# Attention in a streaming-encoder layer: reciprocals of row sums made for two score tiles at once, and their probabilities halved behind the second's exponentials

## The chip, the cores and the metric

The kernel runs on one NeuronCore of a Trainium2 chip. A core has five instruction queues that run beside each other: PE (TensorE, matrix products; PEld are its weight loads), DVE (VectorE), ACT (ScalarE), POOL (GpSimd) and SP (SyncE, which here issues all transfers). Each queue is worked off in order, and an instruction that waits holds up what stands behind it on its queue. The metric is the device time of one execution in microseconds, the lower the better.

## The reference

One encoder layer with a sequence of 1024, a width of 1024 and one batch: a conditioning vector gives shift, scale and gate; two groups of eight heads attend side by side; a gated channel part with a causal convolution of width 3 follows. Cut to what the change is about:

```python
def mla_attention(q, k, v):                # latent attention: 8 heads, 96 wide
    # query blocks of 128; a key is seen if its chunk of 64 is not later than the query's
    s = einsum(q_block, k) * scale;  s = where(mask, s, -1e30)
    p = softmax(s);  return einsum(p, v)

def chunk_attention(q, k, v, rel_bias):    # chunk attention: 8 heads, 64 wide
    # chunks of 64 queries; each sees a band of its own chunk and the 8 before it
    s = einsum(q_chunk, k_band) * scale + bias(rel_bias)
    p = softmax(s);  return einsum(p, v_band)

mixed = concat([o_mla, o_ca]) @ w_out;  x = x + g_a * mixed
```

A softmax row is exp(s - max) divided by its sum. Everything is float32.

## The kernel before

**Number format.** Products are made in three passes: each operand is split into a high and a low half, and high x high, high x low and low x high are added. For the probabilities both halves are float16.

**Stages.** (1) The conditioning and the first projection (to about 85 us). (2) Chunk attention: 8 heads x 8 score tiles = 64 tiles, about 85 to 374 us. (3) Latent attention: 8 heads x 8 tiles = 64 tiles, about 401 to 624 us. (4) The output product and the channel part, from about 630 us to the end. A score tile is 128 queries of one head against all the keys that they may see. Tile i of a head is 128 x (i+1) wide in latent attention, up to 1024; in chunk attention it is 128, 256, 384, 512 and then 640 wide. Each head is worked in two units of four tiles.

**One score tile** (`Unit.scores`): PE makes the scores in PSUM (tag S, two buffers; L765 and L771). DVE masks and takes the row minimum of the negated scores (L778 to L786 in chunk attention; L789 and L790 in latent attention). ACT writes the exponentials to a tile P and their row sums to `rsum` (L797). P has three buffers for tiles up to 640 wide; wider ones use a pool of six pages. DVE makes the reciprocal of the row sum (L799) and multiplies it by a power of two, PSCALE (L800). For each piece of the tile (one piece, or two of at most 512 for latent tiles wider than 512) POOL writes the high half, P times the reciprocal, in float16 (L73, the helper `scale_pool`), DVE the low half, P times the reciprocal minus the high half (L819), both to a tile hl (four buffers, one latent piece in four elsewhere). Then SP issues one transposing transfer of both halves into a tile PT (L831).

**Value product** (`Unit.values`): for a pair of neighbouring tiles, an even one and the odd one behind it, PE multiplies the transposed halves with the values (L859). PT holds both tiles of the pair. After two pairs DVE and ACT combine the result (L868, L869) and SP stores it (L873).

**Order of the work.** The main loop goes over the 128 tiles. Step n makes the scores of tile n, and the value product of tile n-3 if that is the odd one of its pair. After each of the two, `pace` puts in work from a list of fillers in proportion to the PE time of the tile: projections during chunk attention, then the latent projection, the up-projections and the part of the output product that belongs to chunk attention. The instructions of each engine are then ordered by a planner with an estimated timeline: what is ready goes in the order of the program, but the blocks under `high_priority` count as further ahead by an offset, 400 places for scores and exponentials, 200 for the reciprocals, halves and transposes, 200 for the value products. That order is fixed when the program is built; at run time each queue only waits for what it needs.

The steps that the change touches are in these functions:

Of the kernel before, what the change touches and what calls it, by code (L numbers as in the profile page):

```python
# [13 lines left out]
F32 = mybir.dt.float32  # L14
# [4 lines left out]
AF = mybir.ActivationFunctionType  # L19
# [3 lines left out]
MUL, ADD, SUB, MIN, MAX = ALU.mult, ALU.add, ALU.subtract, ALU.min, ALU.max  # L23

P = 128
# [16 lines left out]
OFF_S, OFF_P, OFF_V = 400, 200, 200  # L42
# [3 lines left out]
PSCALE, VSCALE = 2.0 ** 15, 2.0 ** 14  # L46
# [18 lines left out]
def layer_kernel(ctx, tc, I, out):  # L65
    nc = tc.nc
    pe, act, dve, pool, sp = nc.tensor, nc.scalar, nc.vector, nc.gpsimd, nc.sync
# [4 lines left out]
    def scale_pool(o, i, s):  # L72
        pool.tensor_scalar(o, i, s, 1.0, op0=MUL, op1=MUL)  # L73
# [12 lines left out]
    cst = ctx.enter_context(tc.tile_pool(name="cst", bufs=1))  # L86
# [60 lines left out]
    def pgtile(shape, dt, name):  # L147
        return apg.tile(shape, dt, name=name, tag="pg", bufs=6)
# [585 lines left out]
    class Unit:  # L734
# [7 lines left out]
        def scores(u, i):  # L742

            qpg, kpgs = u.pages()
            bias = u.bias() if u.band else None
            lo = max(0, i - 4) if u.band else 0
            n = (i - lo + 1) * P
            nm = f"{u.nm}_{i}"
            rsum = cst.tile([P, 1], F32, name=f"rs{nm}", tag="rsum", bufs=4)
            ri = cst.tile([P, 1], F32, name=f"ri{nm}", tag="ri", bufs=4)  # L750
            with tc.high_priority(offset=OFF_S):
                s = ps.tile([P, 1024], F32, name=f"s{nm}", tag="S", bufs=2)
                n0 = max(0, min(4, i + 1) - lo) * P
                n1 = n - n0
                c0 = 512 - n0 if n1 else 0
                segs = [(c0, lo * P, n0, 0)] if n0 else []
                if n1:
                    segs.append((512, max(lo, 4) * P - 512, n1, 1))
                q = slice((i % 4) * P, (i % 4 + 1) * P)
                rs_ = slice(u.base, u.base + u.rows)  # L760
                if u.band:
                    qh, ql = qpg
                    for a, rr in ((qh[u.odd], slice(0, P)), (ql, rs_)):
                        for c, ko, w, kh in segs:
                            last = pe.matmul(s[:, c:c + w], a[rr, q], kpgs[kh][rr, u.odd, ko:ko + w],  # L765
                                             start=(a is not ql), stop=(a is ql))
                else:
                    for a in range(2):
                        for c, ko, w, kh in segs:
                            for b in range(2 - a):  # L770
                                last = pe.matmul(s[:, c:c + w], qpg[a][rs_, q], kpgs[kh][rs_, b, ko:ko + w],  # L771
                                                 start=(a == 0 and b == 0), stop=(a == 1))
                trail.append(last.ins)
                sv = s[:, c0:c0 + n]
                m = cst.tile([P, 1], F32, name=f"m{nm}", tag="m", bufs=4)
                if u.band:
                    if i >= 4:
                        dve.memset(sv[64:128, 0:64], BIG)  # L778
                    w = min(n, 256)
                    if n > 256:  # L780
                        m0 = cst.tile([P, 1], F32, name=f"m0{nm}", tag="m0", bufs=4)
                        dve.tensor_reduce(m0[:], sv[:, :n - 256], axis=AX.X, op=MIN)
                        init = m0[:]
                    else:
                        init = 3e38
                    anchor["dve"] = dve.tensor_tensor_reduce(sv[:, n - w:n], sv[:, n - w:n], bias[:, 256 - w:256], 1.0, init,  # L786
                                             ADD, MIN, accum_out=m[:]).ins
                else:
                    dve.memset(sv[0:64, n - 64:n], BIG)  # L789
                    anchor["dve"] = dve.tensor_reduce(m[:], sv, axis=AX.X, op=MIN).ins  # L790
                short = n <= (640 if u.band else 512)
                pieces = [(0, n)] if short else [(0, 512), (512, n)]
                if n <= 640:
                    pr = at.tile([P, 640], F32, name=f"P{nm}", tag="P", bufs=P_BUFS)
                else:
                    pr = pgtile([P, 1024], F32, f"P{nm}")
                act.activation(pr[:, :n], sv, AF.Exp, bias=m[:], scale=-1.0, accum_out=rsum[:, 0:1])  # L797
            with tc.high_priority(offset=OFF_P):
                dve.reciprocal(ri[:], rsum[:, 0:1])  # L799
                dve.tensor_scalar(ri[:], ri[:], PSCALE, None, op0=MUL)  # L800
                for x, (p0, p1) in enumerate(pieces):
                    w = p1 - p0
                    cnt[0] += 1
                    if not u.band and cnt[0] % 4 == 0:
                        hl = apg.tile([P, 1024], F16, name=f"hl{nm}_{x}", tag="v16", bufs=3)
                    else:
                        hl = at.tile([P, 1280], F16, name=f"hl{nm}_{x}", tag="HL", bufs=HL_BUFS)
                    pp = pr[:, p0:p1]
                    mode = (MODE_C if u.band else MODE_M)[cnt[0] % 4]
                    if mode == "2":  # L810
                        scale_pool(pp, pp, ri[:])
                        act.activation(hl[:, :w], pp, AF.Copy)
                        pool.tensor_tensor(hl[:, w:2 * w], pp, hl[:, :w], op=SUB)
                    else:
                        if mode == "1":
                            scale_pool(hl[:, :w], pp, ri[:])
                        else:
                            act.activation(hl[:, :w], pp, AF.Copy, scale=ri[:])
                        dve.scalar_tensor_tensor(hl[:, w:2 * w], pp, ri[:], hl[:, :w], op0=MUL, op1=SUB)  # L819
                    nb = 10 if u.band else 8  # L820
                    if i % 2 == 0:
                        pair[0] += 1
                        if u.band or pair[0] % 2:
                            tt = at.tile([P, 20, P], F16, name=f"PT{nm}_{x}", tag="PT", bufs=2)
                        else:
                            tt = apg.tile([P, 16, P], F16, name=f"PT{nm}_{x}", tag="v16", bufs=3)
                        u.pt[i, x] = tt, {}
                    tt, where = u.pt[i - i % 2, x]
                    b0 = (i % 2) * nb
                    with tc.issue_after(anchor["om"]) if u is units[-1] and i == 7 else contextlib.nullcontext():  # L830
                        anchor["sp"] = sp.dma_start_transpose(tt[:, b0:b0 + 2 * w // P, :], hl[:, :2 * w]).ins  # L831
                    for j in range(w // P):
                        where.setdefault(lo + p0 // P + j, []).append((b0 + j, b0 + j + w // P, i % 2))
            return sum(3 * max(107, w / 2.4) for _, _, w, _ in segs)

        def values(u, i):

# [146 lines left out]
    for n in range(len(tiles) + DEPTH):  # L984
        if n < len(tiles):
            u, i = tiles[n]
# [4 lines left out]
        if n >= DEPTH:  # L991
            u, i = tiles[n - DEPTH]
# [613 lines left out]
```

## Time and profile before

| | us |
|---|---|
| runs | 1340.53, 1341.02, 1343.16; median 1341.02 |
| the profiled execution | 1345.89 |
| its span, first to last instruction | 1344.1 |
| PE busy in it | 1223.8 (91%) |
| DVE busy | 1096.2 (82%) |
| ACT busy | 622.7 (46%) |
| POOL busy | 578.1 (43%) |
| mean granted clock of PE | 0.946 |

The profile is of one execution. In its rows L797 is line 797 of the kernel, `out<-in` names the tiles written and read (buffer numbers are left out: Pc and hlc belong to chunk attention, Pm and hlm to latent attention), shapes are partitions x elements. In a group of instructions the first number behind the bar is the busy time in us and the second the mean of one in ns; behind the second bar stands the idle time of the engine just before these instructions, and what ended it. In the order of time a row begins with start and duration in us; `x3` means that three instructions are drawn together, and a bracket tells how long the engine had idled and what ended that. "SPq" is SP's queue of transfers. The granted clock is 1 at full speed.

### The profile page before, as it was taken

How to read it: one execution, taken by the hardware profiler on the slowest of the kernel's cores; microseconds unless marked ns; L12 is line 12 of the kernel's file. 1: busy time of each engine (PE TensorE's matmuls, PEld its weight loads, DVE VectorE, ACT ScalarE, POOL GpSimd, SP SyncE). 2: the span in 40 equal slices, each digit the busy share in tenths (PEclk: the TensorE clock that was granted, in tenths of full speed). 3: DMA queues.
4: the chain of work that ended last, by engine and by line, in shares of the span. 5: the costliest groups of instructions: out<-in, count | busy, mean ns of one | idle time of the engine just before them, and what ended most of it. 6: DMA issues, size and time to landing. Idle time of an engine off the chain costs nothing.

```text
span 1344.1 us, 18696 instructions
## 1 busy us (share of the span) xinstructions
PE 1223.8 (91%) x6168; PEld 1003.8 (75%) x6168; DVE 1096.2 (82%) x1928; ACT 622.7 (46%) x1132; POOL 578.1 (43%) x610
## 2 busy tenths in 40 slices
PE   4899798998877798886998999999999998999998
PEld 3788587896655567765776888888888886888886
DVE  6978798864679987894989988988899997687667
ACT  4453546443555544563376444444434444433431
POOL 5464557565646763354634444444445431000000
PEclk9899798998787889996999999999999998999999
DMA  8415577854413477779911333333323326943441
GB/s 323 138 35 116 135 177 179 192 127 110 87 32 80 94 153 165 141 150 252 377 49 47 126 110 133 103 122 98 133 102 118 126 98 241 390 141 117 130 161 63
DMA packets 223689, 190.57 MB, mean 142 GB/s; under 512 B 148708, under 2 KB 166884, under 8 KB 223592
## 3 DMA queue, kind: packets, MB, share of 16 engines
q1 hardware_dynamic: 223592, 189.38, 49.1%
q8 instruction: 48, 0.79, 0.2%
q14 instruction: 49, 0.40, 0.1%
HBM read 117.24 MB, written 37.49 MB: 115 GB/s over the span
## 4 chain that ended last, share of the span: by engine, by line
PE 41%; DVE 10%; issue 3%; ACT 2%; DMA 1%; POOL 1%; SPq 0%; DVEq 0%; ACTq 0%; POOLq 0%
PE p L1082 7%; PE p L1084 7%; PE p L1083 7%; PE dnA_P L1417 2%; PE dnA_P L1419 2%; PE dnA_P L1418 2%; PE dnB_P L1419 1%; PE dnB_P L1418 1%; PE dnB_P L1417 1%; DVE u L1253 1%; DVE u L1254 1%; PE op L154 1%; PE dnA L1417 1%; PE dnA L1419 1%; PE dnA L1418 1%
## 5 line engine op out<-in xcount | busy, mean ns | idle before, releaser
L77 ACT ACTIVATE dnP<-dnr 128x1024 fp32r<-128x1024 f32 x73 | 77.5, 1064 | 117.5 <-PE dnA_P L1419 46.4
L1391 DVE TENSOR_TENSOR dnP<-dnr,dnP 128x1024 fp32r<-128x1024 f32 x72 | 87.9, 1223 | 52.6 <-ACT dnP L77 52.6
L73 POOL TENSOR_SCALAR hlm<-Pm,rim 128x512 f16<-128x512 f32 (+3 forms) x96 | 68.8, 726 | 83.5 <-DVE rim L800 22.3
L84 POOL TENSOR_TENSOR wf<-wu,wf 128x512 fp32r<-128x512 f32 x22 | 38.8, 1762 | 116.3 <-ACT wf L77 116.3
L1253 DVE SCALAR_TENSOR_TENSOR u<-c,cvp,u 128x1023 f32<-128x1023 f32 x44 | 64.8, 1513 | 27.8 <-ACT u L1252 27.8
L73 POOL TENSOR_SCALAR hlc<-Pc,ric 128x640 f16<-128x640 f32 (+2 forms) x64 | 50.8, 797 | 61.0 <-ACT Pc L797 20.8
L819 DVE SCALAR_TENSOR_TENSOR hlm<-Pm,rim,hlm 128x512 f16<-128x512 f32 (+3 forms) x96 | 68.0, 719 | 9.8 <-POOL hlm L73 9.7
L797 ACT ACTIVATE Pc<-sc,mc 128x640 f32<-128x640 f32 (+2 forms) x64 | 42.1, 658 | 53.1 <-DVE mc L786 35.9
L797 ACT ACTIVATE Pm<-sm,mm 128x128 f32<-128x128 f32 (+3 forms) x64 | 47.1, 736 | 41.7 <-DVE mm L790 24.2
L84 POOL TENSOR_TENSOR wb<-wu,wb 128x512 fp32r<-128x512 f32 x22 | 38.1, 1732 | 64.5 <-ACT wb L77 50.7
L1252 ACT ACTIVATE u<-c,cvp 128x1024 f32<-128x1024 f32 x44 | 52.3, 1237 | 27.8 <-DVE c L1351 19.2
L1254 DVE SCALAR_TENSOR_TENSOR u<-c,cvp,u 128x1022 f32<-128x1022 f32 x44 | 63.8, 1488 | 0.0
L859 PE MATMUL pvm<-PTm,vt 128*128 128x256 f16 (+1 forms) x320 | 45.7, 294 | 17.0 <-DMA PTm<-hlm 9.9
L819 DVE SCALAR_TENSOR_TENSOR hlc<-Pc,ric,hlc 128x640 f16<-128x640 f32 (+2 forms) x64 | 51.6, 809 | 9.3 <-POOL hlc L73 8.7
L155 PE MATMUL ipq<-wq_s,hT 128*128 128x256 f32 x192 | 56.0, 292 | 0.1
L859 PEld LDWEIGHTS <-vt 128*128 128x128 f16 x320 | 31.6, 109 | 32.7 <-DMA PTm<-hlm 15.0
L154 PE MATMUL ipq<-wq_s,hT 128*128 128x256 f32 x192 | 55.8, 293 | 0.0
L156 PE MATMUL ipq<-wq_s,hT 128*128 128x256 f32 x192 | 55.4, 289 | 0.0
L77 ACT ACTIVATE wc<-ws 128x512 fp32r<-128x512 f32 x21 | 13.3, 632 | 88.0 <-DVE ws L1101 82.2
L1418 PE MATMUL dnA_P<-dnP 128*128 128x512 f32 x132 | 51.4, 389 | 0.0
L1419 PE MATMUL dnA_P<-dnP 128*128 128x512 f32 x132 | 51.3, 389 | 0.0
L1417 PE MATMUL dnA_P<-dnP 128*128 128x512 f32 x132 | 51.2, 389 | 0.0
(442 smaller groups left out, 4428.4 us busy)
## 6 DMA issues: line engine op xcount, KB each, us to landing
wu<-w_up SPq DMA_DIRECT2D x44, 512.0 KB, 3.5
dnr<-g_d SPq DMA_DIRECT2D x73, 256.0 KB, 2.8
aw<-w_ada SPq DMA_DIRECT2D x48, 256.0 KB, 3.5
g_d<-u SPq DMA_DIRECT2D x22, 512.0 KB, 3.0
dnr<-w_down SPq DMA_DIRECT2D x44, 256.0 KB, 5.3
adaw<-w_ada_a SPq DMA_DIRECT2D x16, 512.0 KB, 6.3
x<-x SPq DMA_DIRECT2D x16, 512.0 KB, 9.0
g_d<-gs SPq DMA_DIRECT2D x22, 256.0 KB, 2.8
```

The lines of the kernel that those rows point to most:

```text
L73: pool.tensor_scalar(o, i, s, 1.0, op0=MUL, op1=MUL)
L77: act.activation(o, i, AF.Copy)
L797: act.activation(pr[:, :n], sv, AF.Exp, bias=m[:], scale=-1.0, accum_out=rsum[:, 0:1])
L819: dve.scalar_tensor_tensor(hl[:, w:2 * w], pp, ri[:], hl[:, :w], op0=MUL, op1=SUB)
L1082: pe.matmul(pt, sh, pg[:, 0], start=(k == 0 and not add), stop=False, skip_group_check=skip)
L1083: pe.matmul(pt, sh, pg[:, 1], start=False, stop=False, skip_group_check=skip)
L1084: last = pe.matmul(pt, sl, pg[:, 0], start=False, stop=(k == 3), skip_group_check=skip)
L1253: dve.scalar_tensor_tensor(u[:, 1:], c[:, :S - 1], cvp[:, cv + 1:cv + 2], u[:, 1:], op0=MUL, op1=ADD)
L1391: r = f(*a, **k)
L1417: pe.matmul(pt, sh, w[:, 0, 0], start=start, stop=False, skip_group_check=add)
L1418: pe.matmul(pt, sh, w[:, 1, 0], start=False, stop=False, skip_group_check=add)
L1419: pe.matmul(pt, sl, w[:, 0, 0], start=False, stop=stop, skip_group_check=add)
```

## The change

The row sums of an even tile and the odd tile behind it now lie in the two columns of one tile. `scores` ends with the exponentials and notes the tile down; behind the odd tile's exponentials it calls a new function, `weigh`. That makes one reciprocal and one scaling over both columns, and then calls `halve` for the even tile and for the odd tile. `halve` holds the lines for halves and transposes as they were, and takes its column of the reciprocals. The pair of row sums and the pair of reciprocals have two buffers each instead of four single ones. Tiles, halves and transposes are otherwise of the same kind and number.

```diff
-            rsum = cst.tile([P, 1], F32, name=f"rs{nm}", tag="rsum", bufs=4)
-            ri = cst.tile([P, 1], F32, name=f"ri{nm}", tag="ri", bufs=4)
+            if i % 2 == 0:
+                u.rs = cst.tile([P, 2], F32, name=f"rs{nm}", tag="rsum", bufs=2)
+                u.todo = []
+            rsum = u.rs[:, i % 2:i % 2 + 1]
...
-                act.activation(pr[:, :n], sv, AF.Exp, bias=m[:], scale=-1.0, accum_out=rsum[:, 0:1])
+                act.activation(pr[:, :n], sv, AF.Exp, bias=m[:], scale=-1.0, accum_out=rsum)
+            u.todo.append((i, nm, pr, pieces, lo))
+            if i % 2:
+                u.weigh()
+            return sum(3 * max(107, w / 2.4) for _, _, w, _ in segs)
+
+        def weigh(u):
+
+            rr = cst.tile([P, 2], F32, name=f"ri{u.todo[0][1]}", tag="ri", bufs=2)
             with tc.high_priority(offset=OFF_P):
-                dve.reciprocal(ri[:], rsum[:, 0:1])
-                dve.tensor_scalar(ri[:], ri[:], PSCALE, None, op0=MUL)
+                dve.reciprocal(rr[:], u.rs[:])
+                dve.tensor_scalar(rr[:], rr[:], PSCALE, None, op0=MUL)
+            for i, nm, pr, pieces, lo in u.todo:
+                ri = rr[:, i % 2:i % 2 + 1]
+                u.halve(i, nm, pr, pieces, lo, ri)
+
+        def halve(u, i, nm, pr, pieces, lo, ri):
+
+            with tc.high_priority(offset=OFF_P):
                 for x, (p0, p1) in enumerate(pieces):
...
-                            scale_pool(hl[:, :w], pp, ri[:])
+                            scale_pool(hl[:, :w], pp, ri)
...
-                        dve.scalar_tensor_tensor(hl[:, w:2 * w], pp, ri[:], hl[:, :w], op0=MUL, op1=SUB)
+                        dve.scalar_tensor_tensor(hl[:, w:2 * w], pp, ri, hl[:, :w], op0=MUL, op1=SUB)
...
                         anchor["sp"] = sp.dma_start_transpose(tt[:, b0:b0 + 2 * w // P, :], hl[:, :2 * w]).ins
...
-            return sum(3 * max(107, w / 2.4) for _, _, w, _ in segs)
```

More of the change, by code (lines that the diff above doesn't have):

```diff
@@ L810, in scores @@
                     if mode == "2":
-                        scale_pool(pp, pp, ri[:])
+                        scale_pool(pp, pp, ri)
                         act.activation(hl[:, :w], pp, AF.Copy)
@@ L815, in scores @@
                         if mode == "1":
-                            scale_pool(hl[:, :w], pp, ri[:])
+                            scale_pool(hl[:, :w], pp, ri)
                         else:
-                            act.activation(hl[:, :w], pp, AF.Copy, scale=ri[:])
-                        dve.scalar_tensor_tensor(hl[:, w:2 * w], pp, ri[:], hl[:, :w], op0=MUL, op1=SUB)
+                            act.activation(hl[:, :w], pp, AF.Copy, scale=ri)
+                        dve.scalar_tensor_tensor(hl[:, w:2 * w], pp, ri, hl[:, :w], op0=MUL, op1=SUB)
                     nb = 10 if u.band else 8
```

## The prediction, made before the result was known

> **What bounds the kernel now.** I read the page's span and busy times first, then the table of busy time by stretch, then, for the operations that the change touches, the groups by line and shape, the waits of the attention tiles, and last the order of time of single pairs of score tiles.
>
> ```profile
> span 1344.1 us, 18696 instructions
> ...
> PE 1223.8 (91%) x6168; PEld 1003.8 (75%) x6168; DVE 1096.2 (82%) x1928; ACT 622.7 (46%) x1132; POOL 578.1 (43%) x610
> ```
>
> PE is busy for most of the span, but that is an average. The next table cuts the span into chunk attention (85 to 374 us), the latent attention while the up-projection still fills in (401 to 480), the latent attention with the output product as filler (480 to 600), its end without filler (600 to 624), and the channel part behind it. Columns: length, PE, PEld, DVE, ACT and POOL busy with counts, granted PE clock, DMA share, GB/s.
>
> ```profile
> 85.00:374.00 289.00, 263.34 (x1663) 223.95 (x1664) 213.94 (x611) 136.37 (x349) 164.96 (x238) 0.90 0.59 136
> ...
> 401.00:480.00 79.00, 57.48 (x267) 44.31 (x266) 74.20 (x215) 45.74 (x109) 56.34 (x56) 0.77 0.43 95
> 480.00:600.00 120.00, 109.06 (x625) 86.67 (x626) 99.78 (x258) 61.66 (x129) 53.17 (x69) 0.97 0.74 152
> 600.00:624.00 24.00, 14.47 (x80) 10.49 (x79) 18.13 (x40) 10.15 (x20) 13.32 (x16) 0.81 0.81 179
> 640.00:1344.00 704.00, 687.70 (x3013) 560.41 (x3011) 595.85 (x592) 307.76 (x411) 224.18 (x156) 0.99 0.41 141
> ```
>
> Three regimes. In chunk attention PE leads (263 of 289) and DVE has a quarter of its time free. From 401 to 480 DVE leads (74.2 of 79) and PE waits at a granted clock of 0.77. From 480 to 600 PE leads again (109 of 120) with DVE close behind (99.8). The 704 us behind 640 are PE at 98%, and the change does not touch them. So the change can win or lose only in the latent attention, some 223 us. Does PE wait there for the halves that the change moves? These rows of the views of the transposed halves (PT) tell who waited for them (us, times), in the latent attention and then in chunk attention:
>
> ```profile
>   PEld L859: 15.0, 10
>   PE pvm L859: 9.9, 8
> ```
>
> ```profile
>   PEld L859: 2.8, 3
>   PE pvc L859: 2.3, 4
> ```
>
> In chunk attention the halves come early (2.3 us of matmul waits in 289); in the latent attention the value product already starts as the last transpose lands. A later last transpose is covered in the first and bare in the second.
>
> **The change part by part.** *Removed:* 64 of 128 reciprocals and 64 of 128 scalings on DVE.
>
> ```profile
> L799 DVE RECIPROCAL rim<-rsm 128x1 f32<-128x1 f32 x64 | 9.7, 151 | 4.5 <-ACT Pm L797 4.3
> ...
> L800 DVE TENSOR_SCALAR rim<-rim 128x1 f32<-128x1 f32 x64 | 9.2, 143 | 0.5
> ```
>
> The pair's instruction handles two columns instead of one. No row shows that width; it lies between the same 0.15 us and twice that (at twice nothing is saved), and one column more is nearer to the one column of these rows, so I take the same. The next rows are the reciprocals alone by stretch (length, busy, count, clock, DMA share, GB/s).
>
> ```profile
> 85.00:374.00 289.00, 9.52 (x64) 0.90 0.59 136
> 401.00:480.00 79.00, 2.65 (x18) 0.77 0.43 95
> 480.00:600.00 120.00, 6.11 (x40) 0.97 0.74 152
> 600.00:624.00 24.00, 0.92 (x6) 0.81 0.81 179
> ```
>
> Half of the reciprocals go, and as many scalings. In chunk attention that is 32 x (0.149 + 0.143) = 9.3 us, worth nothing while PE leads there (9.3 at most if it did not). In the latent attention it is 32 x 0.294 = 9.4 us, worth what DVE is on the path: 9 x 0.294 = 2.6 us in the first, where DVE leads, taken whole; 20 x 0.294 = 5.9 in the second, where PE leads, taken at a fifth, 1.2; 3 x 0.294 = 0.9 in the third, taken at half, 0.4. Sum **-4.2**, ends -9.4 and 0 (-18.7 if chunk attention paid too).
>
> *Moved:* scale on POOL (L73), low half on DVE (L819) and transpose on SP (L831) of each even tile now wait for the odd tile's exponential (L797). What is lost is the head start. In 18 of 32 latent pairs the first POOL scale starts before the odd tile's exponential is through, and in 8 the first DVE half does. The first and the last of the 18, each with its second exponential (the rows stand by engine: POOL, ACT, DVE):
>
> ```profile
> 426.96 2.31 POOL L73 TENSOR_SCALAR hlm<-Pm,rim 128x512 f16<-128x512 f32 x2 [0.63 <-issue]
> ...
> 612.63 1.14 POOL L73 TENSOR_SCALAR hlm<-Pm,rim 128x512 f16<-128x512 f32 x2 [2.21 <-DVE sm L789]
> 614.63 1.35 POOL L73 TENSOR_SCALAR hlm<-Pm,rim 128x384 f16<-128x384 f32 x1 [0.85 <-DMA PTm<-hlm]
> 618.29 0.69 POOL L73 TENSOR_SCALAR hlm<-Pm,rim 128x512 f16<-128x512 f32 x1 [2.32 <-DVE rim L800]
> ...
> 430.20 0.90 ACT L797 ACTIVATE Pm<-sm,mm 128x768 f32<-128x768 f32 x1
> ...
> 614.45 1.11 ACT L797 ACTIVATE Pm<-sm,mm 128x1024 f32<-128x1024 f32 x1 [1.37 <-DVE mm L790]
> ...
> 614.86 1.91 DVE L819 SCALAR_TENSOR_TENSOR hlm<-Pm,rim,hlm 128x512 f16<-128x512 f32 x3
> 616.69 0.15 DVE L799 RECIPROCAL rim<-rsm 128x1 f32<-128x1 f32 x1
> ...
> 619.02 0.75 DVE L819 SCALAR_TENSOR_TENSOR hlm<-Pm,rim,hlm 128x512 f16<-128x512 f32 x1 [0.98 <-POOL hlm L73]
> ```
>
> So in the other 14 pairs the queues already do what the change asks. The last pair shows both signs: the even tile's halves (614.86, three passes) sit in front of the odd tile's reciprocal, which starts at 616.69 though the exponential ended at 615.56; with the change the pair's reciprocal takes that place first. Price of the lost start: the nearest rows are the POOL scale and DVE half of the commonest piece.
>
> ```profile
> L819 DVE SCALAR_TENSOR_TENSOR hlm<-Pm,rim,hlm 128x512 f16<-128x512 f32 x48 | 43.1, 897 | 6.9 <-POOL hlm L73 6.8
> ...
> L73 POOL TENSOR_SCALAR hlm<-Pm,rim 128x512 f16<-128x512 f32 x48 | 41.6, 868 | 61.2 <-DVE rim L800 14.5 <-DVE sm L789 10.5 <-ACT Pm L797 8.4
> ```
>
> Upper end: one scale in each of the 18 pairs comes wholly late, 18 x 0.868 = 15.6 us. Lower end: 0, because after the second exponential a scale every 0.7 us feeds a transpose every 1.3 us, so that POOL and DVE catch up behind the first piece. Behind the waiting scale stand on POOL the norm powers of the filler (L120), whose q and k wait for them; behind the waiting half on DVE the minima of the next tiles (L790), whose exponentials wait. The scores are drawn 400 places ahead in the order and the halves 200, so the minima go first where they are ready; what is left I count within this term. I take **+3**, near the lower end, because 14 of 32 pairs pay nothing and the odd tile's reciprocal moves up in others.
>
> *Transposes on SP in one run.* Behind one pair SP now issues two (small tiles) or four (large ones) without a break. It already does so at places:
>
> ```profile
> 614.56 5.33 SPq L831 DMA_TRANSPOSE PTm<-hlm  x4
> 619.98 0.54 SPq L873 DMA_DIRECT2D oT_d<-om  x1
> 620.62 2.68 SPq L831 DMA_TRANSPOSE PTm<-hlm  x2
> ```
>
> Four cost 5.3 us of SP's queue. Loads of weights and latent outputs that were planned between the even and the odd tile's transposes now stand up to 2.7 us later behind them, or come ahead of them: **+0.5**, ends -1 and +3. At the end of attention the last pair's first transpose could start about 615.6 + 0.15 + 0.14 + 0.69 + 0.75 = 617.3 at best, and three more at 1.34 end at 622.7; now the last two end at 620.62 + 2.68 = 623.3 behind another store. I take **+0.3**, ends -0.6 and +1.3 (one transpose).
>
> *Buffers.* The probability tile P (three buffers up to 640 wide) of the even tile is held until the pair is weighed, so the exponential three tiles on can wait for one DVE half more. Nearest row 0.9 us; of the chain through exponentials I take **+0.5**, ends 0 and +3. The row sums and reciprocals keep the same number of columns, no price.
>
> *Two engines at once.* The last two-sided cost is that the odd tile's POOL scale now runs beside the even tile's DVE half. Quoted above: a 512-wide scale takes 0.69 at 618.29 with no DVE half beside it, 0.868 on average; a 512-wide half 0.75 at 619.02 alone, 0.897 on average. They already meet often. If all 32 latent pairs gained one meeting on the path it would cost 32 x (0.18 + 0.15) = 10.6 us. Large tiles meet already inside their own two pieces, which leaves the 16 pairs of small tiles, 5.3 us; of these I take a little over a quarter, **+1.5**, since POOL is off the path. Ends 0 and +10.6. [...]
>
> Sum: -4.2 + 3 + 0.5 + 0.3 + 0.5 + 1.5 = **+1.6 us**. The profiled execution took 1345.9 us (span 1344.1), 4.9 above the median of the three runs, 1341.0. On it the sum makes 1347.5, on the median 1342.6, which I round to 1343. A measurement of this kernel tells 0.2%, 2.7 us, from no change.
>
> **The rivals.** *Slower by the lost head start.* The value product in the latent attention has no slack (24.9 us of PT waits), so the scales of the 18 pairs come late in full: +15.6 - 4.2 = +11.4, 1352. It decides from the point where the waits on PT grow past some 30 us. For it: those waits, and a DVE that at 74 of 79 us cannot catch up. Against: in 14 pairs nothing moves, and DVE has fewer instructions. [...]
>
> *Faster.* DVE paces the whole latent attention, the 9.4 us come off the path, and of the other terms only 2 us of the head start remain: 1341.0 - 7.4 = 1333.6. For it: DVE at 94% from 401 to 480. Against: PE at 91% from 480 to 600. Here belongs the case that the change does not do what it says, because most even halves ran behind the second exponential anyway: then only the -4.2 are left, 1337.
>
> *Slower by contention.* All 32 pairs pay one more meeting in full, +10.6 - 4.2 = +6.4, 1347, with DVE passes longer than before and no new wait on PT.
>
> **How the numbers follow.** Forecast (a wash, 1338 to 1347) 0.42, of which 0.30 lie within 0.2%, 0.02 under and 0.10 over it; lost head start 0.28, slower; faster or without the move 0.22; contention 0.08, slower. That makes faster 0.24, same 0.30, slower 0.46. The range runs from the faster case to just past the first slower one, 1332 to 1354; beyond it I leave below 2 in 10, mostly for orders of the queues that come out otherwise than now, since the planner draws them anew from the first score tile on.
>
> **What would show it.** Reciprocals and scalings x64 in all, at 0.15 us. Latent attention from its first exponential (401 us) to the last transpose (623 us) as long as now within 4 us, and everything behind it as long as now. PT waits of the latent attention between 25 and 30 us; more speaks for the first rival. The mean 512-wide scale and half within 0.05 us of 0.868 and 0.897; 0.1 more speaks for contention. DVE busy down by some 15 to 19 us from 1096. The prediction is wrong if chunk attention changes its length, by exponentials waiting for P or by PE running out of filler: I hold that at nothing.

## The result and the profile after

The changed kernel takes **1356.84 us** (median of six runs, 1348.57 to 1358.97) against 1341.36 for the kernel before (six runs, 1340.51 to 1344.78). The ratio of the means is **1.0102, 95% interval 1.0072 to 1.0131**, which is 13.7 us slower (9.7 to 17.6); the medians stand 15.5 apart. Forecast were 1343, with a range of 1332 to 1354. Below, a difference is always that ratio less one, times the median of the kernel before on the same chip in the same session; its interval stands in brackets.

One execution each was profiled: 1345.89 us before and 1353.63 after, 7.7 apart. The one lies 4.5 above its median and the other 3.2 below, so the two profiles can place only about half of the difference. The head of the page of the changed kernel:

```profile
span 1351.8 us, 18531 instructions
...
PE 1220.3 (90%) x6168; PEld 1000.6 (74%) x6168; DVE 1089.4 (81%) x1800; ACT 624.2 (46%) x1132; POOL 577.3 (43%) x610
```

The 128 small VectorE instructions are gone (1928 to 1800). The table of busy time by stretch, cut as in the prediction (length, PE, PEld, DVE, ACT and POOL busy, granted clock, DMA share, GB/s), of the changed kernel:

```profile
85.00:374.00 289.00, 259.21 (x1641) 219.42 (x1641) 211.96 (x538) 134.59 (x347) 160.24 (x238) 0.91 0.59 134
401.00:480.00 79.00, 54.62 (x263) 41.25 (x264) 74.64 (x206) 47.51 (x113) 54.02 (x54) 0.79 0.39 86
480.00:600.00 120.00, 105.25 (x590) 83.88 (x587) 96.19 (x208) 59.77 (x122) 53.53 (x67) 0.95 0.71 150
600.00:624.00 24.00, 20.40 (x118) 16.07 (x118) 19.73 (x41) 13.16 (x28) 13.37 (x16) 1.00 0.80 172
```

PE does less in each of the first three stretches (4.1, 2.9 and 3.8 us less than before): work is pushed back, and the end of attention is fuller because it still has that work to do. Exponentials mark how far attention has come. First the kernel before (order of time, ScalarE: exponentials number 23 and 31 of the chunk attention, counted from 0, and the first of the latent attention; its last one, at 614.45, stands in the prediction):

```profile
183.74 0.69 ACT L797 ACTIVATE Pc<-sc,mc 128x512 f32<-128x512 f32 x1 [1.63 <-DVE mc L786]
...
218.54 0.79 ACT L797 ACTIVATE Pc<-sc,mc 128x640 f32<-128x640 f32 x1
...
401.35 0.37 ACT L797 ACTIVATE Pm<-sm,mm 128x128 f32<-128x128 f32 x1
```

Then the same, with the last of the latent attention, of the changed kernel:

```profile
182.40 0.69 ACT L799 ACTIVATE Pc<-sc,mc 128x512 f32<-128x512 f32 x1 [0.87 <-DVE mc L788]
...
224.01 0.80 ACT L799 ACTIVATE Pc<-sc,mc 128x640 f32<-128x640 f32 x1
...
405.07 0.37 ACT L799 ACTIVATE Pm<-sm,mm 128x128 f32<-128x128 f32 x1
...
625.04 1.11 ACT L799 ACTIVATE Pm<-sm,mm 128x1024 f32<-128x1024 f32 x1
```

The changed kernel is 1.3 us ahead at 182, 5.5 behind at 224, 3.7 behind at the start of the latent attention and 10.6 behind at its last exponential. So in these two profiles the chunk attention, which the prediction held at nothing, loses some 4 us, and the latent attention some 7; what follows the last exponential is 2.9 us shorter, which leaves the 7.7. The loss of the chunk attention falls between 190 and 210. There the table by stretch says of the kernel before and then of the changed one:

```profile
190.00:200.00 10.00, 10.00 (x70) 8.06 (x69) 9.05 (x25) 5.11 (x11) 6.08 (x7) 1.00 0.71 161
200.00:210.00 10.00, 6.05 (x27) 4.21 (x25) 9.03 (x23) 8.42 (x26) 7.72 (x9) 0.78 0.59 148
```

```profile
190.00:200.00 10.00, 5.56 (x34) 4.05 (x33) 7.52 (x22) 7.80 (x23) 4.14 (x7) 0.92 0.60 151
200.00:210.00 10.00, 7.93 (x29) 5.77 (x29) 7.88 (x17) 5.27 (x15) 6.99 (x7) 0.50 0.83 169
```

Both kernels run out of filler whose weights are ready at this place, the changed one earlier and longer, and then its granted clock is 0.50 for ten microseconds, where the kernel before had 0.78. What PE waits for there (order of time of the changed kernel, PE) is a split weight of the next projection:

```profile
194.56 0.61 PE L767 MATMUL sc<-k,ql 64*128 64x128 f32 x2
198.76 0.58 PE L154 MATMUL ipv<-wv_s,hT 128*128 128x256 f32 x1 [3.59 <-ACT wv_s L77]
```

That late halves held this weight up is not shown: its load starts at 194.94 in the changed kernel and at 200.87 in the kernel before, and there PE waits for the same split too.

In the latent attention the waits on the transposed halves have grown. The view of PT in the changed kernel, who waited for it (us, times):

```profile
  PE pvm L875: 22.4, 12
  PEld L875: 16.3, 11
```

That is 38.7 us against 24.9, past the 30 from which the first rival of the prediction was to decide. But the sign does not tell a lost head start from a new order. The same view of e18, an experiment below that adds no dependency and is as slow:

```profile
  PE pvm L876: 26.7, 13
  PEld L876: 19.7, 11
```

These are 46.4 us; e6, without a dependency too, has 40.7. And e7, the changed kernel with another offset, has 17.2 and is no faster.

### The profile page after: what moved, and what is told of

Read it like the earlier page. It is cut to its first block, busy times and chain, and to the rows that moved or that the text cites. A ratio compares the mean times of both kernels' runs of the same rounds, so it can differ in the third digit from the quotient of the medians.

```text
span 1351.8 us, 18531 instructions
## 1 busy us (share of the span) xinstructions
PE 1220.3 (90%) x6168; PEld 1000.6 (74%) x6168; DVE 1089.4 (81%) x1800; ACT 624.2 (46%) x1132; POOL 577.3 (43%) x610
## 4 chain that ended last, share of the span: by engine, by line
PE 50%; DVE 3%; issue 1%; DMA 0%; SPq 0%; POOL 0%; ACT 0%; DVEq 0%; POOLq 0%
PE p L1100 10%; PE p L1099 10%; PE p L1098 10%; PE dnA_P L1433 2%; PE dnA_P L1435 2%; PE dnA_P L1434 2%; PE dnB_P L1435 1%; PE dnB_P L1434 1%; PE dnB_P L1433 1%; PE op L154 1%; PE op L155 1%; PE op L156 1%; PE dnA L1433 1%; PE dnA L1434 1%; PE dnA L1435 1%
## 5 line engine op out<-in xcount | busy, mean ns | idle before, releaser
L77 ACT ACTIVATE dnP<-dnr 128x1024 fp32r<-128x1024 f32 x73 | 77.2, 1061 | 117.0 <-PE dnA_P L1435 46.4
L73 POOL TENSOR_SCALAR hlm<-Pm,rim 128x512 f16<-128x512 f32 (+3 forms) x96 | 71.9, 761 | 72.2 <-ACT Pm L799 16.5
L1269 DVE SCALAR_TENSOR_TENSOR u<-c,cvp,u 128x1023 f32<-128x1023 f32 x44 | 59.2, 1386 | 27.8 <-ACT u L1268 27.8
L836 DVE SCALAR_TENSOR_TENSOR hlm<-Pm,rim,hlm 128x512 f16<-128x512 f32 (+3 forms) x96 | 68.7, 736 | 10.6 <-POOL hlm L73 10.5
L84 POOL TENSOR_TENSOR wb<-wu,wb 128x512 fp32r<-128x512 f32 x22 | 41.0, 1863 | 72.1 <-ACT wb L77 56.7
L73 POOL TENSOR_SCALAR hlc<-Pc,ric 128x640 f16<-128x640 f32 (+2 forms) x64 | 44.0, 699 | 48.3 <-ACT Pc L799 16.9
L875 PEld LDWEIGHTS <-vt 128*128 128x128 f16 x320 | 31.1, 106 | 38.8 <-issue 19.6
```

What stands on the lines that cost most here:

```text
L77: act.activation(o, i, AF.Copy)
L84: (pool if eng == "p" else dve).tensor_tensor(o, i, f32(hi), op=SUB)
L836: dve.scalar_tensor_tensor(hl[:, w:2 * w], pp, ri, hl[:, :w], op0=MUL, op1=SUB)
```

## The experiments

All 18 were timed beside the kernel before. Two kinds of edit return: the planner is left *free* to order the queues anew, as it was for the changed kernel, or the order is *held*. Holding works so: every instruction except the named ones is chained to the one that precedes it on its engine in the program of another kernel. The chain fixes the order of issue and adds no wait.

```diff
+def _hold_order(tc):
+    nosync = mybir.DependencyInfo(mybir.DependencyClass.NoSync, mybir.DependencyReason.DATA)
...
+    for e, order in json.loads(zlib.decompress(base64.b85decode(_ORDER))).items():
...
+                tc.add_manual_dep(seq[e][at], seq[e][last].name, nosync, reason="order")
```

| run | what | planner | median us | difference us |
|---|---|---|---|---|
| the changed kernel | pair everywhere | free | 1356.84 | +13.7 [9.7, 17.6] |
| e1 | pair in chunk attention only | free | 1346.10 | +3.1 [0.9, 5.1] |
| e2 | pair in latent attention only | free | 1346.16 | +2.7 [0.4, 5.0] |
| e3 | halves emitted later, nothing merged | free | 1349.25 | +6.7 [4.3, 9.1] |
| e4, e5, e6 | kernel before, offset 50, 140, 300 | free | 1356.03, 1346.05, 1353.46 | +12.2 [9.3, 15.3], +2.7 [0, 5.2], +8.7 [7.1, 10.5] |
| e7 | changed kernel, offset 400 | free | 1359.53 | +15.2 [13.4, 16.9] |
| e8 | changed kernel, last four tiles singly | free | 1353.66 | +10.3 [8.5, 12.2] |
| e9 | pair everywhere | held, before | 1385.90 | +43.4 [41.2, 45.5] |
| e10, e11 | pair in chunk, in latent attention only | held, before | 1354.97, 1366.60 | +12.5 [10.3, 14.6], +23.2 [19.9, 26.6] |
| e12 | halves emitted later, nothing merged | held, before | 1357.11 | +13.8 [10.3, 17.5] |
| e13 | 128 scalings left out, nothing moved | held, before | 1335.21 | -7.4 [-9.8, -5.1] |
| e14 | kernel before | held, changed | 1365.03 | +22.3 [19.6, 24.8] |
| e15 | dependency, nothing merged | held, before | 1383.16 | +40.0 [37.6, 42.4] |
| e16 | dependency, nothing merged | free | 1354.02 | +11.6 [8.7, 14.5] |
| e17 | first tile's transposes late only | held, before | 1356.62 | +14.3 [10.3, 18.4] |
| e18 | 128 scalings left out, nothing moved | free | 1355.49 | +13.4 [9.7, 17.2] |

### Which half of attention (e1, e2)

The theories were lost head start in the latent attention (as in the prediction's first rival), a loss in the chunk attention, and a loss by the new order of the queues whatever is moved. In both runs `weigh` works on the tiles noted down so far, one or two.

```diff
-            if i % 2:
+            if i % 2 or not u.band:        # e2: if i % 2 or u.band
                 u.weigh()
```

> The pair is kept in the chunk attention and taken out of the latent attention, whose tiles get their reciprocal, scaling and halves each behind its own exponentials, as before. If the loss is the latent attention's lost head start (the place that the prediction named), this kernel stands within 4 us of before, 1338 to 1345 us. If the loss comes from the chunk attention, where the profile of the changed kernel is some 4 us behind by the 31st tile, it stands 4 to 8 us above before, 1345 to 1349. If any new order of the queues costs this much, whatever is moved, it stands anywhere up to the changed kernel's 1357.

> The reverse: the pair in the latent attention alone. Lost head start in the latent attention: 1350 to 1358 us, all of the loss or nearly. Loss in the chunk attention: 1340 to 1347. If the two parts add, this and the run with the pair in the chunk attention alone lie above before by amounts whose sum is about 15 us.

Measured: +3.1 and +2.7. Neither half has the loss; together they make 5.8 of 13.7. The latent attention alone is far from the 11 that lost head start would have cost there, so that theory fell in the form in which it was put. Two parts that do not add up suggest something that both share.

### The move without the merging (e3), and places without a dependency (e4 to e7)

```diff
+            with tc.high_priority(offset=OFF_P):
+                dve.reciprocal(u.rr[:, c], rsum)
+                dve.tensor_scalar(u.rr[:, c], u.rr[:, c], PSCALE, None, op0=MUL)
             if i % 2:
                 u.weigh()
```

> The move alone: every tile gets its own reciprocal and scaling behind its own exponentials, as before, and only the halves of both tiles stand behind the second's. All 64 pairs of small VectorE operations are back (the sum put them at 4.2 us of gain when merged). Lost head start: 1357 to 1362 us, the changed kernel's time plus 0 to 4. If the wait of the merged reciprocal for the second tile is itself what costs, and not the later halves, the time falls back to 1341 to 1345.

```diff
-OFF_S, OFF_P, OFF_V = 400, 200, 200
+OFF_S, OFF_P, OFF_V = 400, 50, 200      # e4; e5 140; e6 300; e7 400, on the changed kernel
```

> The kernel before with one number changed: the planner's head start for reciprocals and halves is 50 in place of 200, so that each tile's halves stand later in the queues, with no new dependency and no operation changed. If the loss of the changed kernel is one of places in the queues, and any reordering of this extent costs it, 1348 to 1360 us. If the dependency on the second tile is needed for it, 1338 to 1346.

> The kernel before, with the planner's head start for reciprocals and halves at 140 in place of 200: a small new order of the same operations with the same dependencies (at 50 it cost 12 us). If a new order is a draw that costs several us either way, the time lies anywhere from 1336 to 1356. If only late halves cost, and 140 is nearly what 200 is, 1339 to 1346.

> The same with 300: the halves are planned earlier than in the kernel before. A draw: 1336 to 1356, and no order among 50, 140, 200 and 300. Lateness of the halves as the cause: 1336 to 1342, at or below before, since they are earlier.

> The changed kernel with the head start at 400 in place of 200, so that the halves, though still behind the second tile's exponentials, get places in the queues as early as that allows. If the loss is that the even tile's halves are planned a step later, 1342 to 1349. If the loss is the dependency itself (the head start that the even tile no longer has), 1353 to 1360, as the changed kernel. A draw of the order: anywhere from 1342 to 1360.

e3 gave +6.7, below what was expected of a move that still costs the head start. The expectation read the edit too strictly: the first tile's halves come later in the program, but they need only their own factor, so this kernel has late places and no dependency. e4 to e6 have no new dependency at all and cost 12.2, 2.7 and 8.7: 50, 140, 200 and 300 give no order by lateness, since the halves are earlier at 300 than at 200. None of the other three is faster than the kernel's own, 200. So in this kernel an order that the planner draws anew, with the same operations, can cost as much as the change did. e7 shows that an earlier place does not help the changed kernel.

### The end of attention (e8)

```diff
-            if i % 2:
+            if i % 2 or u is units[-1]:
                 u.weigh()
```

> The changed kernel with the last group of eight score tiles done tile by tile as before, all else as changed. In the profiles the changed kernel loses 7 to 9 us in that group (its last exponentials come 10.6 us later, 7 us more than those of the group before it). If that is the end of attention and not a scatter of one profile, the time falls by 5 to 9 us, to 1348 to 1352. If not, it stays at 1354 to 1359.

The edit reaches less than the expectation says: the last unit is four tiles, not eight. Measured +10.3, 3.3 less than the changed kernel, with overlapping intervals; whether the last pairs cost anything of their own stays unclear.

### The dependency with all else held (e9 to e12)

Here TensorE and ScalarE issue exactly what the kernel before issues, in its order; on VectorE, GpSimd and SyncE only reciprocals, scalings, halves and transposes may stand elsewhere. The theories: the loss is the new order (then holding removes it), or the dependency of the first tile's halves on the second tile (then it stays).

```diff
     with tile.TileContext(nc, schedule_with_timeline_sim=True) as tc, ExitStack() as ctx:
         layer_kernel(ctx, tc, I, out)
+        _hold_order(tc)
```

> The changed kernel with everything but the moved operations (reciprocals, scalings, halves and their transposes) held in the order in which the kernel before issues it, engine by engine: TensorE's and ScalarE's queues are then the same in both kernels, and VectorE's, GpSimd's and SyncE's differ in the moved operations alone. If the loss is the new order of the rest of the work, 1337 to 1345 us (the sum's own terms remain: -4.2 for the removed operations, 0 to +6 for late halves). If the loss is the dependency of the first tile's halves on the second tile, 1351 to 1360 us. Between, each has its part.

> The same with the pair in the chunk attention alone (left free, this cost 3.1 us). New order as the cause: 1339 to 1344. The dependency as the cause: 1345 to 1349.

> The same with the pair in the latent attention alone (left free, 2.7 us). New order: 1338 to 1344. The dependency: 1345 to 1356, since here the prediction put the lost head start.

> The move alone (reciprocals and scalings per tile, halves of both tiles behind the second), the rest held in the order of the kernel before (left free, 6.7 us). Against the held pair it differs by the merged operations only: if their removal is worth the 4.2 us of the sum, it stands 3 to 5 us above the held pair; if VectorE's small operations are hidden, within 2 us of it.

Measured: +43.4, +12.5, +23.2 and +13.8. No theory had expected three times the loss. The pair costs in both halves of attention, and here the halves nearly add up (35.7 of 43.4). For e12 the expectation was wrong as for e3: it has later places and no dependency, so it stands 29.6 below the held pair, and its 13.8 are the price of the later places in this order. Held to the order of the kernel before, the changed kernel waits wherever that order counted on the first tile's halves; the planner's new order takes some 30 us of this back. Where the waits are, is in the waits of the two kernels during attention (engine, line, what it waited for: us in total, times, longest). The kernel before:

```profile
POOL hlm L73 <- ACT Pm L797: 10.4, 5, 4.1
ACT wo L77 <- DMA wor<-w_out: 10.2, 2, 9.9
...
ACT ch L77 <- DMA cl<-oT_d: 9.7, 5, 3.8
...
ACT wq_s L77 <- DMA wq_r<-w_qk: 5.0, 6, 1.6
```

And e9, whose lines stand 23 (splits and scales), 25 (exponentials), 41 (value product) and 42 (low halves, transposes) further down:

```profile
POOL hlm L96 <- ACT Pm L822: 33.5, 7, 9.4
...
PEld L900 <- DMA PTm<-hlm: 22.9, 13, 4.5
PE pvm L900 <- DMA PTm<-hlm: 21.0, 16, 4.1
...
ACT ch L100 <- DMA cl<-oT_d: 17.5, 6, 5.7
...
ACT wo L100 <- DMA wor<-w_out: 14.2, 3, 5.4
...
ACT wq_s L100 <- DMA wq_r<-w_qk: 12.4, 7, 4.6
```

Three engines wait longer by these rows. GpSimd stands at scales until exponentials are there (33.5 us for 10.4), with the splits of filler weights behind it. This row is one releaser of several: all the idle time of GpSimd ahead of the latent scales is 89.8 us for 83.5, so it grew by 6.3 and not by 23.1. PE waits longer for PT (43.9 for 24.9). And ScalarE waits longer for loads (these three make 44.1 for 24.9). SyncE issues those loads, and its own waits, for low halves before it can issue their transposes, show what they stand behind. The kernel before, and then e9:

```profile
SPq L831 <- DVE hlc L819: 63.9, 23, 14.5
SPq L831 <- DVE hlm L819: 26.0, 14, 5.4
```

```profile
SPq L873 <- DVE hlc L861: 84.5, 27, 16.5
SPq L873 <- DVE hlm L861: 49.3, 27, 5.4
```

### Is it the dependency or the merging (e15, e16)

Both keep a reciprocal and a scaling per tile and emit the halves of both tiles behind the second's exponentials, as e12 and e3 do. What they add is that the first tile's scale on GpSimd waits for the second's factor.

```diff
+                u.last = dve.tensor_scalar(u.rr[:, c], u.rr[:, c], PSCALE, None, op0=MUL)
...
-                            scale_pool(hl[:, :w], pp, ri)
+                            scaled = pool.tensor_scalar(hl[:, :w], pp, ri, 1.0, op0=MUL, op1=MUL)
+                            if i % 2 == 0:
+                                tc.add_manual_dep(scaled.ins, u.last.ins.name, mybir.DependencyInfo(
+                                    mybir.DependencyClass.Sync, mybir.DependencyReason.DATA), reason="second")
```

> All else held in the order of the kernel before, a reciprocal and a scaling per tile (nothing merged), but the scaling of the first tile's P on GpSimd made to wait for the second tile's factor. Against the held pair (+43 us) it lacks only the merging, against the held move (+14 us) it has the dependency more. Late halves as the cause: 1375 to 1388 us, as the held pair. The merged VectorE operations and their place as the cause: 1352 to 1362, as the held move.

> The same dependency with reciprocals and scalings per tile, nothing held: the changed kernel without its merging. If merging is worth the sum's 4.2 us, 1358 to 1364 us. If it is worth nothing, as the changed kernel, 1353 to 1359. If the merging is what costs, as the move alone, 1346 to 1352.

Held, the later places and the dependency together cost 40.0 of the 43.4, and the later places alone 13.8 (e12). Free, they cost 11.6 of 13.7, and the later places alone 6.7 (e3). So under the held order the late halves are the cause. Left free, the order is drawn anew in each of these kernels, and how much of the 13.7 comes by the late halves is not shown (e18 below). The merged operations bring nothing that can be seen in either: the kernels with 128 operations less are not faster in either pair.

### What the removed operations are worth, and what an order is worth (e13, e18, e14)

```diff
-PSCALE, VSCALE = 2.0 ** 15, 2.0 ** 14
+PSCALE, VSCALE = 1.0, 2.0 ** 14
...
-                dve.tensor_scalar(rr[:, c], rr[:, c], PSCALE, None, op0=MUL)
```

> The kernel before, per tile, with the 128 scalings by 2^15 left out (the factor is set to 1 and the halves are that much smaller) and everything else, halves too, held in the order of the kernel before. As many small VectorE operations go as the change removes, with nothing moved and no dependency added: the price of the sum's first term, -4.2 us, by itself. If the term is right, 1336 to 1340 us; if VectorE's small operations are hidden behind other waits, 1341 to 1344.

> The kernel before without the 128 scalings by 2^15 (factor 1), nothing else changed and nothing held: the planner is free to order anew. Held, this took 7.4 us off. If a new order is a draw that costs several us whatever the change, 1338 to 1350 us. If only added dependencies and late places cost, 1333 to 1337, as held.

> The operations and dependencies of the kernel before, with all but reciprocals, scalings, halves and transposes held in the order in which the changed kernel issues it: TensorE's and ScalarE's queues are the changed kernel's. If the 13.7 us of the changed kernel are the price of its order, 1351 to 1358 us. If they are waits for the late halves under an order that is in itself as good, 1340 to 1346.

e13 takes 7.4 us off, more than the 4.2 of the term, and is the only kernel of the study that beats both: 128 small VectorE operations have about that price where nothing else moves. No run holds the kernel before and changes nothing, and e13 also makes the halves smaller numbers; that neither has a part in the 7.4 is assumed. e18 issues the same instructions as e13 in an order that the planner drew anew, and stands 13.4 above the kernel before, above both of its answers. The heads of the two pages, e13 and then e18:

```profile
span 1332.4 us, 18530 instructions
...
PE 1209.8 (91%) x6168; PEld 992.3 (74%) x6168; DVE 1088.1 (82%) x1800; ACT 622.0 (47%) x1132; POOL 582.2 (44%) x610
```

```profile
span 1354.1 us, 18549 instructions
...
PE 1223.8 (90%) x6168; PEld 1007.8 (74%) x6168; DVE 1081.3 (80%) x1800; ACT 622.5 (46%) x1132; POOL 577.7 (43%) x610
```

The counts on every engine are the same, VectorE is even less busy in e18, and the medians are 20.3 us apart. That is the price of an order alone, and it arises in attention: the last exponential starts at 602.6 in e13 and at 627.7 in e18. e14, the kernel before in the order of the changed kernel, costs 22.3, more than either theory allowed and 8.6 more than the changed kernel in that order. By e9 and e14 each order is dear with the dependencies of the other kernel, so the 13.7 cannot be divided into so much for the order and so much for the dependency.

### By which queue (e17)

```diff
-                        anchor["sp"] = sp.dma_start_transpose(tt[:, b0:b0 + 2 * w // P, :], hl[:, :2 * w]).ins
+                    u.late.append((i, tt[:, b0:b0 + 2 * w // P, :], hl[:, :2 * w]))
...
+                    if i % 2 == 0:
+                        tc.add_manual_dep(anchor["sp"], u.last.name, mybir.DependencyInfo(
+                            mybir.DependencyClass.Sync, mybir.DependencyReason.DATA), reason="second")
```

> The kernel before, every engine's order held and halves made per tile as soon as before, but the transposes of each first tile wait for the second tile's scaling factor (on SyncE; the transposes alone are free to move in its queue). If the 40 us of the held dependency come by SyncE, through transposes that land late and through loads that stand behind them, 1370 to 1385 us. If they come by GpSimd and VectorE, whose queues stand behind the late halves, 1342 to 1355.

Measured +14.3, some third of the 40.0 of e15, 1.6 us above the second answer. GpSimd idles 84.7 us ahead of the latent scales, little more than in the kernel before (83.5), and PE waits less for PT, but a load of the latent outputs comes late (17.2 us for 9.7):

```profile
ACT ch L100 <- DMA cl<-oT_d: 17.2, 6, 9.5
...
PEld L914 <- DMA PTm<-hlm: 12.3, 8, 3.8
...
PE pvm L914 <- DMA PTm<-hlm: 8.2, 9, 3.5
```

So late transposes on SyncE are the smaller part, and through what stands behind them; the other 26 us come only when the halves on GpSimd and VectorE are late too. Which of those two engines has more of it was not tried.

## Why the prediction was wrong

**The failed step is the term "moved", taken at +3 with ends 0 and +15.6.** Its mechanism stood in the prediction, and as the first rival (chance 0.28), but its size was wrong. Moving the halves behind the second tile, with nothing merged, measured +11.6 [8.7, 14.5] where the planner was free (e16) and +40.0 with all else in the order from which the prediction took its rows (e15). The term priced the direct lateness, one scale of 0.868 us in each of 18 latent pairs as its upper end. What stands behind a late half on the queues was named, and then "what is left I count within this term". In e9 that part is seen in loads and value products that come late. And the -4.2 for the removed operations, which the sum set against it, did not show: the changed kernel is no faster than e16.

**The step that is missing is a price for the new order.** The prediction left under 2 in 10 for a time beyond its range, mostly for "orders of the queues that come out otherwise than now", and no term of the sum. Such orders cost 2.7 to 12.2 us without any change of operations, and 20.3 us lie between e13 and e18. The 11.6 of e16 hold such a new order too. The changed kernel's 13.7 have the size of the 13.4 of e18, whose new order serves no new dependency. So the runs show that the moved halves are dear in the old order, and that a new order alone can cost as much as was measured; which of the two made the 13.7 stays open.

The first rival's +11.4 lies inside the measured interval, but by luck: it put the whole loss into the latent attention, and the pair there alone costs 2.7 left free (e2) and 23.2 held (e11).

Point by point:

- *Chunk attention is worth nothing.* Wrong. The pair there costs 3.1 free and 12.5 held. That PE leads with 263 of 289 us did not cover the change: where PE stood still longest between 190 and 210, it waited for a split filler weight. That the late halves held up such weights is argued, not shown.
- *Removed, -4.2, ends -9.4 and 0.* As many operations gone in place measured -7.4 (e13), within the ends; merged they showed no gain. The assumption that two columns cost what one does holds for the reciprocal and for most scalings; in the views of the reciprocals and of VectorE's groups of the changed kernel:

```profile
L809 DVE RECIPROCAL rim<-rsm x32: 141/151/167, 408.6 to 626.5; 128x2 f32<-128x2 f32 x32
L810 DVE TENSOR_SCALAR rim<-rim x32: 149/168/1116, 409.3 to 626.9; 128x2 f32<-128x2 f32 x32
...
L810 DVE TENSOR_SCALAR rim<-rim 128x2 f32<-128x2 f32 x32 | 8.0, 249 | 0.4
```

(The three numbers behind `x32:` are the shortest, the median and the longest, in ns.) The median reciprocal has 0.151 us, the mean of one column was 0.151. The scaling has a median of 0.168 for a mean of 0.143, but a mean of 0.249, because some take up to 1.116 us; the last section shows what ran beside those. So 64 scalings fewer save VectorE 3.3 us in the whole kernel and 64 reciprocals fewer 9.2, together 12.5 of the 18.7 that the prediction counted. The gain of the merging was never free of the dependency, and did not show (e9 beside e15, the changed kernel beside e16).

- *Transposes in one run, +0.5, ends -1 and +3.* Too small, under the held order: late transposes alone cost 14.3 there (e17).
- *End of attention, +0.3.* Not settled (e8).
- *P buffers, +0.5, ends 0 and +3.* Not tried by itself, but the waits passed its end. Exponentials waited 2.4 us for a P tile to come free in the kernel before, and 14.9 in the changed kernel:

```profile
ACT Pc L799 <- DVE hlc L836: 5.4, 3, 2.7
...
ACT Pm L799 <- DVE hlm L836: 4.8, 6, 1.7
...
ACT Pc L799 <- POOL hlc L73: 2.6, 1, 2.6
...
ACT Pm L799 <- POOL hlm L73: 2.1, 2, 1.4
```

The free kernels with the dependency everywhere have 14.5 to 15.0 us of them (the changed kernel, e7, e16). The free kernels without it have 0.6 to 6.7 (e3 to e6, e18), and e9, the slowest, has 4.6. So these waits come with the dependency where the planner is free, but they do not follow the loss: e18 is as slow with 6.7. What part of them is on the path is not shown.

- *Contention of GpSimd and VectorE, +1.5.* Not seen as a cause. The groups of the 512-wide halves and scales in the changed kernel:

```profile
L73 POOL TENSOR_SCALAR hlm<-Pm,rim 128x512 f16<-128x512 f32 x48 | 43.5, 907 | 49.2 <-ACT Pm L799 14.3 <-ACT co L686 9.5 <-ACT om L884 7.0
L836 DVE SCALAR_TENSOR_TENSOR hlm<-Pm,rim,hlm 128x512 f16<-128x512 f32 x48 | 38.5, 804 | 4.4 <-POOL hlm L73 4.3
```

The scale is 0.04 us longer and the half 0.09 shorter than before; 0.1 more on both was the sign.

- *Signs named beforehand.* Of these, 64 reciprocals and 64 scalings came as said. Latent attention as long as now within 4 us did not: its last exponential is 6.9 us later counted from its first. PT waits passed 30, but this does not decide for the first rival, since e18 and e6 pass it without the dependency. Chunk attention changed its length, and exponentials waited for P, both named as signs of being wrong. VectorE's busy time fell by 6.8, not 15 to 19: the merged operations saved 12.5, and other operations of VectorE took longer and shorter in the two executions, for which no run settles why.

What stays open: how the 13.7 divide between the late halves and the new order; which feature of an order costs the microseconds, that is, what makes the order that the planner drew for e18 so much dearer than e13's; and how much of the changed kernel's 13.7 a better order could still take back.

## What to carry to other kernels

When one operation is made to serve two tiles, price what the first tile loses by waiting for the second: all that stands behind its late work on every queue, in the stages with slack too, and not only the work itself. Where a planner orders the queues, time a change twice, once with everything untouched held in its old order and once free: here the same instructions took 1335 and 1355 us. And look first for a way to remove the small operations that adds no dependency: 128 of them gone in place were worth 7.4 us, while as many gone by merging were worth nothing that could be measured.

## What the runs showed of the hardware

**In these kernels a scaling of two columns that began during a GpSimd pass over a wide tile (256 elements or more in each partition) ended just after that pass, and one of one column did not take longer.** In the changed kernel 9 of the 64 scalings (128x2) took 0.34 to 1.12 us, the others 0.15 to 0.21. Each of the nine, and no other, began while such a pass ran, and ended 0.02 to 0.03 us after it. The longest, first the pass on GpSimd and then the scaling on VectorE (order of time):

```profile
538.10 1.76 POOL L84 TENSOR_TENSOR cl<-cl,ch 128x512 fp32r<-128x512 f32 x1 [1.71 <-ACT ch L77]
...
538.77 1.12 DVE L810 TENSOR_SCALAR rim<-rim 128x2 f32<-128x2 f32 x1
```

The pass ends at 539.86, the scaling at 539.89. In the kernel before 33 of the 128 scalings of one column began while such a wide pass ran, and none of the 128 took more than 0.155 us. The 12 scalings of the changed kernel that began during narrower GpSimd work (at most 128 elements in each partition, as the norm powers of 128x8, L120) took 0.15 to 0.21 us.

**Executions of one and the same program scattered by up to 13 us** (e5 from 1341.01 to 1354.04, e12 from 1350.50 to 1363.66). Of the changed kernel's six, the shortest span was 1346.8 us at a mean granted clock of 0.952 and the longest 1357.2 at 0.944; the other four lie between at 0.950, 0.946, 0.945 and 0.943 (1351.8, 1356.2, 1353.9, 1356.8). If TensorE's busy time of 1220 us went with the clock, the difference of 0.008 / 0.95 would be worth 10 us, about the scatter of these six; that is an estimate from these numbers. It is no rule: e7's four have clocks of 0.940 to 0.947 and spans within 1.0 us. Whether a few gaps of PE that fall differently set the clock, or the clock itself differs, these runs do not show; e13, the fastest kernel, had 0.963 in its profiled execution and e9, the slowest, 0.940. So single profiles could not measure this change of 1%: those of before and after stood 7.7 us apart, the medians 15.5.
